# The Newton steps of all norms move from GpSimd to VectorE, in a two-block transformer kernel on one core

## The chip, the cores and the metric

The kernel runs on one core of one Trainium2 chip. The metric is the time of one execution on the device in microseconds (us); lower is better. Before the change it is 1208.56 us, the median of three runs (1205.94, 1208.56 and 1211.92). The trace was taken by the hardware profiler in one further execution. In its rows PE is TensorE's matrix multiplications, PEld its weight loads, DVE is VectorE, ACT ScalarE, POOL GpSimd and SP SyncE, which issues most of the transfers.

## The reference, cut to what matters

256 tokens of 1024 columns pass through two blocks of two layers each, all in float32. The first block mixes tokens by three branches (a recurrent one, attention over selected keys, dilated attention) and then has a gated projection; the second has two kinds of attention, attention to a memory of 256 rows, and a feed-forward layer with a short convolution. Each part begins with a norm over the 1024 columns of a token:

```python
def rms_norm(x, g):
    y = x * lax.rsqrt(jnp.mean(x * x, axis=-1, keepdims=True) + 1e-6)
    return y * g

for i in range(2):                                   # first block
    z = rms_norm(x, norm_g[i]) @ w_in[i]
    x = x + mix(z) @ w_out[i]
    x = x + sigmoid(rms_norm(x, ple_norm_g[i]) @ ple_w_gate[i]) * (p[i] @ ple_w_proj[i])
x = rms_norm(x, final_norm_g)
for l in range(2):                                   # second block
    h = rms_norm(x, attn_norm[l])                    # and, once, rms_norm(x, kv_norm)
    x = x + attention(h, rms_norm(mem, mem_norm[l])) @ w_o[l]
    x = x + conv_ffn(rms_norm(x, ffn_norm[l]), w_up[l], w_down[l])
out = rms_norm(x, final_norm)
```

## The kernel before, in words

The tokens lie in two tiles of 128 rows, `xs[0]` and `xs[1]`. A matrix product in float32 is made of three products of a rounded part and a remainder (`hi` and `lo`, pass list `PASSES`): weights are loaded as `wraw`, ScalarE copies the rounded part into `whi`, and VectorE, or for some blocks GpSimd, subtracts to get `wlo`. Activations are split likewise (tiles `k`, `mT`). Six slots hold weights ahead of their use.

**A norm.** `norm_T` turns a tile of tokens on TensorE into columns, VectorE multiplies by the gains (`zs`), ScalarE and VectorE (or GpSimd) make the two parts. The factor 1/sqrt(mean square) is not applied there; it scales what the products give. `stats` makes it, for each tile of tokens: ScalarE sums the squares (`squares`), VectorE adds the two halves (`halved`, tile `ss`), and `newton` computes the root from an integer seed on VectorE and three rounds of two steps on [128, 1] tiles: `rs_t` = y·y·h, then y = (t - 1.5)·y, in tile `rs_y` (`mrs` for the norm of the memory). Each step needs the one before it. In the kernel before, the steps go to GpSimd unless `newton` is called with `eng=V`, as only the final norm does (`plain_norm`).

The factor is used in two ways: as a column that ScalarE multiplies rows of tokens with, and spread over a square tile: `spread_rs` has VectorE scale the identity by the factor of each tile of tokens (`diag`), then TensorE multiplies the two `diag` with ones, and ScalarE copies the result to `wide`. Between `diag` and the product, `spread_rs` lets other work be issued for a time that is worked out by an estimate, plus `SPREAD_LAG`, 3.5 us.

There are 20 chains of steps on GpSimd, two (one per tile of tokens) for each of: the entry norms of the two first layers, their gate norms (`ple_norm_g`), the memory's norm, the first feed-forward norm, the entry norm of the last layer, and the last feed-forward norm; and four for the norm that joins the first block's final norm with the second's first one (`norm_norm_stats`). In the gate norms GpSimd then halves the factor.

**The order of the work.** Many streams (generators) are emitted by `Flow.run`, which asks an estimate, `Clock`, when the operands of each will be there, and emits next what can go on. The estimate has a price for each instruction and engine (`RATE` and `note`): by them a step of a chain costs 0.15 + 1/475 + 2 x 0.09 = 0.33 us on GpSimd and 0.069 + 1/1920 + 2 x 0.06 = 0.19 on VectorE, plus 0.125 from one to the next. For TensorE the order of emission is the order of execution (`manual_schedule`); that of the other engines is made by the scheduler of the language from the order of emission. GpSimd's other work is weight splits, some `lo` parts of activations, a few products of the recurrent branch, small memsets and the loads of small parameters.

In the rows L458 is the line in `Timed` through which all instructions of VectorE, ScalarE, GpSimd and SyncE are issued, and L616 and L621 are the matrix product and the transpose.

Of the kernel before, what the change touches and what calls it, by code (L numbers as in the profile page):

```python
# [14 lines left out]
ALU = mybir.AluOpType  # L15
AX = mybir.AxisListType
PSUM = bass.MemoryType.PSUM
# [93 lines left out]
class Ev:  # L111
    """A point in the emission that other streams can wait for."""

# [8 lines left out]
class Fork:  # L122
    """A stream to be started that the one that yields it doesn't wait for."""

# [4 lines left out]
WAIT = object()  # L129
# For each run of streams: the time to allow for what may come in between, and that from or to the tensor engine.  # L130
PACE = ((0.2, 0.2), (0.6, 0.28), (0.2, 0.28), (0.5, 0.22), (0.2, 0.2), (0.15, 0.26), (0.2, 0.28), (0.2, 0.2), (0.2, 0.2))
# [5 lines left out]
class At:  # L137
    """The time when some instructions are through, as far as it can be told."""

# [16 lines left out]
class Clock:  # L156
    """Estimates when the engines are through with what has been emitted.

    An instruction's time follows from its size, its dependences from the regions that it reads and writes. An engine
    that is free starts the first of the instructions that are ready. What lies more than PAST before the present  # L160
    is settled for good.
    """

# [20 lines left out]
    def follows(self, pool, old):  # L184
        """Tiles of a pool take the place of those of an earlier one."""
        self.prior[pool] = self.of_pool(old)
# [16 lines left out]
    def before(self, reads, writes=(), lane=None):  # L203
        """The instructions that one with these operands comes after; engines that read a bank of PSUM take turns."""
        deps = []
        for ap in reads:
            if lane and lane != "PE" and ap.space == PSUM:
                deps += [op for other, op in self.last.get(ap.name, {}).items() if other not in (lane, "PE")]
        for aps, write in ((reads, False), (writes, True)):
            for ap in aps:  # L210
                name, p0, p1, f0, f1 = self.region(ap)
                for q0, q1, g0, g1, op, wrote in self.used.get(name, ()):
                    if (wrote or write) and q0 < p1 and p0 < q1 and g0 < f1 and f0 < g1:
                        deps.append(op)
                if write and name not in self.used:
                    deps += self.prior.get(self.pool.get(name), ())
                if write and name in self.owner and name not in self.used:
                    (key, bufs), live = self.owner[name], self.slots.setdefault(self.owner[name][0], [])
                    if len(live) == bufs:
                        deps += self.last[live.pop(0)].values()  # L220
                    live.append(name)
        return deps
# [92 lines left out]
class Flow:  # L315
    """Orders the emission of several streams of work by an estimate of the tensor engine's time.

    A stream is a generator that emits a step at a time and yields what its next step waits for: WAIT (what it has
    emitted), an Ev, an At, 0, or a list of streams to be run before it goes on. Streams given first come first.
    """  # L320

# [30 lines left out]
    def tensor(self, cycles, out, st, mv):  # L352
        """A product of the tensor engine. Those that fill different columns of the array run at the same time.

        The clock is at its full rate in a window that follows one with enough work, counted in full columns.
        """
        lanes = range(*(x // 32 for x in (self.clock.region(out)[1], self.clock.region(out)[2] + 31)))
        t = start = max(self.issue, self.clock.when("PE", self.clock.before((st, mv), (out,))), *(self.lanes[i] for i in lanes))
        share = st.shape[0] / P
        left = cycles  # L360
        while left > 0:
            k = int(t / TICK + 1e-9)
            rate = 2400 if self.work.get(k - 1, 0) >= BUSY else 1200
            n = min(left, max((k + 1) * TICK - t, 1e-6) * rate)
            self.work[k] = self.work.get(k, 0) + n * share
            t += n / rate
            left -= n
        t += 0.0024
        self.issue = start + 0.02
        for i in lanes:  # L370
            self.lanes[i] = t
        self.t = max(self.t, t)
        self.clock.mark(Op("PE", t - start, (), t), (st, mv), (out,))

    def slack(self):
        """Whether the tensor engine has had too little to do of late to keep its clock up."""
        k = int(self.t / TICK)
# [7 lines left out]
    def mine(self, lag=0.0):  # L385
        """What the present stream has emitted, and some time for what may come in between."""
        s = self.cur
# [60 lines left out]
class Timed:  # L448
    """An engine whose instructions the clock sees."""

# [17 lines left out]
class Gate:  # L468
    """Open when some condition holds."""

# [18 lines left out]
def tile_hybrid_stack(ctx: ExitStack, tc: tile.TileContext, a, out):  # L489
# [25 lines left out]
    def load_gains(names):  # L515
        """The gains of norms as columns, a column for each 128 of the rows of the matrices that they scale."""
        n = sum(dict(NORMS)[name] for name in names) * KD
# [163 lines left out]
    class Load:  # L681
        """Weights that are used together, in blocks of what a slot holds."""

# [25 lines left out]
    def loading(u):  # L709
        """Loads and splits weights as slots come free; the units are used in the order in which they are loaded."""  # L710
        if u.after:
# [41 lines left out]
    class Chain:  # L753
        """The weights of a stream in the order of use: the next ones are loaded while some are used."""

# [52 lines left out]
    def proj(mm, n, u, split=False, after=None):  # L808
        """mm makes the products of an output, a row of the weights and its index."""
        for i, b in [(i, b) for b in u.blocks for i in range(n)] if split else [(i, b) for i in range(n) for b in u.blocks]:  # L810
# [58 lines left out]
    class Norm:  # L869
        """The factors of a norm, of which a column scales rows of tokens and the square of a tile columns of tokens."""  # L870

# [13 lines left out]

    def newton(h, tag="rs_y", eng=None):
        """1/sqrt(2 h), with a sign that changes at each step."""
        y = T([P, 1], tag)
        t = T([P, 1], "rs_t")
        ts(y.bitcast(I32), h.bitcast(I32), -0.5, float(0x5F3759DF - (1 << 22) - (1 << 31)), ALU.mult, ALU.add)  # L890
        for _ in range(3):
            ts(t, y, y, h, ALU.mult, ALU.mult, eng or G)
            ts(y, t, 1.5, y, ALU.subtract, ALU.mult, eng or G)
        return y
# [9 lines left out]
    def spread_rs(nr, tag, halves_=False):  # L904
        """The factors along the columns, in all rows."""
        dgs = []
# [25 lines left out]
    def turned_T(xh, t, outs, pool=False):  # L932
        """Puts the transpose of a tile of tokens, scaled by the columns of the gains named in outs, into their stacks."""
        for j in range(2):
# [21 lines left out]
    def norm_norm_stats(x_ev, g1, nr, dst):  # L956
        """xs becomes its norm with g1, and nr has the factors of both that and the norm of it.

        The two factors 1/sqrt(s) and 1/sqrt(q/s + eps), with s and q the mean squares of x (plus eps) and of x g1,
        make 1/sqrt(q + eps s).  # L960
        """
        gb1 = load_gain(g1)
# [31 lines left out]
    def scores(pair):  # L994
        """Of two heads on the two halves of the partitions, whose products the array makes side by side."""
        got = yield from take_n(phase["score"])
# [73 lines left out]
    def scaled(ps, nr, n=2):  # L1070
        """Products of n x 128 rows with tokens along the columns, times the factors of the norm of the tokens."""
        x = T([P, 2, S], "zs")[:, 0:n]
# [11 lines left out]
    def rows(accs, yT, u, t, first, last, toks=None, x_ev=None, turns=True):  # L1084
        """Products of a tile of rows with all the blocks of u, into the two banks in accs, to be added to xs in the end."""
        for b in u.blocks if turns else sorted(u.blocks, key=lambda b: b.cols.start):
# [13 lines left out]
    def out_proj(yT, chain, groups, tags, x_ev):  # L1100
        """Adds the products of a group of rows at a time, so that two banks are enough while the last rows are made."""
        for i, ks in enumerate(groups):
# [1294 lines left out]
    def plain_norm(g, x_ev):  # L2397
        gb = load_gain(g.rearrange("(o n) -> o n", o=1))

        def one(t):  # L2400
# [4 lines left out]
            for j in range(2):  # L2405
                tt(xg[j], xh[j], column(gb)[j], ALU.mult)
            rs = newton(halved(s2), eng=V)
            for j in range(2):
# [123 lines left out]
```

## Time and profile before

| What | Value |
|---|---|
| Median of three runs | 1208.56 us |
| Span of the profiled execution, first to last instruction | 1214.1 us |
| A time of that execution beside its span | not given |
| Instructions | 23478 |
| TensorE busy (products) | 92% |
| VectorE busy | 76% |
| ScalarE busy | 60% |
| GpSimd busy | 30% |
| Mean granted clock of TensorE | 0.956 |

Busy shares are means over the whole span. What one stage loses is read from the waits in that stage: a row such as "PE po <- DVE diag: 5.5, 1, 5.5" says that TensorE stood idle for 5.5 us in total, once, and that the last thing it waited for was VectorE's writing of `diag`. In rows in order of time, a row with x2 joins two instructions that follow closely, its time is that of both, and brackets hold the idle time ahead of it and what ended it. Clock columns give the granted clock of TensorE as a share of 2.4 GHz.

### The profile page before, as it was taken

How to read it: one execution, taken by the hardware profiler on the slowest of the kernel's cores; microseconds unless marked ns; L12 is line 12 of the kernel's file. 1: busy time of each engine (PE TensorE's matmuls, PEld its weight loads, DVE VectorE, ACT ScalarE, POOL GpSimd, SP SyncE). 2: the span in 40 equal slices, each digit the busy share in tenths (PEclk: the TensorE clock that was granted, in tenths of full speed). 3: DMA queues.
4: the chain of work that ended last, by engine and by line, in shares of the span. 5: the costliest groups of instructions: out<-in, count | busy, mean ns of one | idle time of the engine just before them, and what ended most of it. 6: DMA issues, size and time to landing. Idle time of an engine off the chain costs nothing.

```text
span 1214.1 us, 23478 instructions
## 1 busy us (share of the span) xinstructions
PE 1123.1 (92%) x8505; PEld 1000.8 (82%) x8505; DVE 928.3 (76%) x2246; ACT 727.0 (60%) x1642; POOL 362.7 (30%) x355
## 2 busy tenths in 40 slices
PE   6899999988989989979989899999989998999996
PEld 6888887888888867978856899999878867999995
DVE  4889887768898877868777677777777666877786
ACT  4526656656266666666556566666666555766664
POOL 4442213433521226160001612222251124222221
PEclk9879989989899999988979999999989999999999
DMA  7444324444452146647312456666534424666662
GB/s 213 111 125 122 80 53 139 139 140 109 119 141 80 45 134 213 194 116 212 101 35 51 153 152 204 192 187 181 185 92 140 139 84 145 183 191 186 188 183 95
DMA packets 154124, 168.60 MB, mean 139 GB/s; under 512 B 15692, under 2 KB 141532, under 8 KB 154008
## 3 DMA queue, kind: packets, MB, share of 16 engines
q1 hardware_dynamic: 153336, 166.10, 46.9%
q0 software_dynamic: 672, 1.00, 0.4%
q8 instruction: 67, 1.10, 0.4%
q14 instruction: 49, 0.40, 0.1%
HBM read 164.65 MB, written 2.42 MB: 138 GB/s over the span
## 4 chain that ended last, share of the span: by engine, by line
PE 64%; issue 13%; DVE 10%; POOL 8%; ACT 4%; DMA 1%; SPq 0%; ACTq 0%; POOLq 0%; DVEq 0%
PE pz L616 34%; PE po L616 9%; PE pr L616 7%; PE sc L616 7%; POOL k L458 4%; PE tp L616 3%; PE tp L621 3%; POOL wlo L458 2%; DVE k L458 2%; DVE wlo L458 2%; ACT whi L458 2%; POOL rs_t L458 1%; POOL rs_y L458 1%; PE pr L621 1%; DVE zs L458 1%
## 5 line engine op out<-in xcount | busy, mean ns | idle before, releaser
L458 ACT ACTIVATE whi<-wraw 128x512 fp32r<-128x512 f32 (+2 forms) x604 | 371.2, 624 | 248.9 <-PE pz L616 72.5
L458 DVE TENSOR_TENSOR wlo<-wraw,whi 128x512 fp32r<-128x512 f32 (+1 forms) x505 | 365.1, 736 | 141.8 <-ACT whi L458 131.7
L616 PE MATMUL pz<-k,whi 128*128 128x256 f32 x1568 | 314.0, 297 | 7.7 <-ACT k L458 4.9
L616 PEld LDWEIGHTS pz<-k,whi 128*128 128x128 f32 x1568 | 255.8, 200 | 18.5 <-issue 5.8
L458 POOL TENSOR_TENSOR wlo<-wraw,whi 128x512 fp32r<-128x512 f32 (+3 forms) x99 | 132.9, 1344 | 415.9 <-ACT whi L458 378.4
L616 PE MATMUL pz<-whi,k 128*128 128x256 f32 (+5 forms) x1152 | 248.9, 302 | 8.4 <-DVE k L458 5.0
L616 PE MATMUL pz<-k,wlo 128*128 128x256 f32 x784 | 229.1, 292 | 10.2 <-POOL wlo L458 10.2
L616 PEld LDWEIGHTS pz<-whi,k 128*128 128x128 f32 (+1 forms) x1152 | 187.2, 188 | 20.3 <-DVE k L458 6.9
L458 POOL TENSOR_TENSOR k<-yv,k 128x256 fp32r<-128x256 f32 x54 | 95.6, 1785 | 280.8 <-ACT k L458 280.8
L616 PE MATMUL pz<-wlo,k 128*128 128x256 f32 (+5 forms) x576 | 170.6, 296 | 0.1
L616 PEld LDWEIGHTS pz<-k,wlo 128*128 128x128 f32 x784 | 157.2, 200 | 11.5 <-POOL wlo L458 11.5
L616 PE MATMUL po<-k,whi 128*128 128x256 f32 x704 | 132.1, 281 | 0.0
L616 PEld LDWEIGHTS pz<-wlo,k 128*128 128x128 f32 (+1 forms) x576 | 108.5, 188 | 3.3 <-DVE wlo L458 0.6
L616 PEld LDWEIGHTS po<-k,whi 128*128 128x128 f32 x704 | 109.0, 191 | 0.0
L616 PE MATMUL po<-k,wlo 128*128 128x256 f32 x352 | 98.8, 281 | 0.0
L616 PE MATMUL sc<-whi,k 128*128 128x512 f32 x240 | 82.2, 402 | 3.8 <-POOL k L458 3.5
L458 DVE SCALAR_TENSOR_TENSOR k<-zs,convp,k 128x254 f32<-128x254 f32 (+1 forms) x176 | 73.7, 482 | 0.0
L458 ACT ACTIVATE sm<-sm,mn 128x128 f32<-128x128 f32 x100 | 44.4, 445 | 37.9 <-DVE mn L458 37.8
L616 PEld LDWEIGHTS po<-k,wlo 128*128 128x128 f32 x352 | 67.0, 190 | 0.0
L616 PE MATMUL tp<-whi,k 128*128 128x512 f32 x176 | 58.8, 395 | 0.0
L616 PEld LDWEIGHTS sc<-whi,k 128*128 128x128 f32 x240 | 45.1, 189 | 15.9 <-POOL k L458 4.8
L616 PE MATMUL sc<-wlo,k 128*128 128x512 f32 x120 | 47.4, 395 | 0.0
(372 smaller groups left out, 1858.5 us busy)
## 6 DMA issues: line engine op xcount, KB each, us to landing
wraw<-in_w_up_dram SPq DMA_DIRECT2D x88, 512.0 KB
wraw<-in_w_in_dram SPq DMA_DIRECT2D x44, 512.0 KB
wraw<-in_w_down_dram SPq DMA_DIRECT2D x44, 512.0 KB
wraw<-in_w_in_dram SPq DMA_DIRECT2D x32, 256.0 KB
wraw<-in_w_out_dram SPq DMA_DIRECT2D x16, 512.0 KB
wraw<-in_ple_w_gate_dram SPq DMA_DIRECT2D x16, 512.0 KB
wraw<-in_w_o_dram SPq DMA_DIRECT2D x10, 512.0 KB
wraw<-in_w_kv_shared_dram SPq DMA_DIRECT2D x10, 512.0 KB
```

The source lines that it names most:

```text
L458: ins = call(*args, **kw)
L616: nc.tensor.matmul(out_, st, mv, start=start, stop=stop)
L621: nc.tensor.transpose(out_, x, idn)
```

## The change

`newton` loses its argument `eng`, and its steps are issued to VectorE, the default of `ts`. The final norm, which passed `eng=V`, is called without it and stays as it was. The halving of the factor in the gate norms stays on GpSimd (`eng=G` in `stats`). Docstrings and a comment are taken out with the lines kept, so line numbers are the same; this part of the diff is left out here.

```diff
-    def newton(h, tag="rs_y", eng=None):
+    def newton(h, tag="rs_y"):
...
         for _ in range(3):
-            ts(t, y, y, h, ALU.mult, ALU.mult, eng or G)
-            ts(y, t, 1.5, y, ALU.subtract, ALU.mult, eng or G)
+            ts(t, y, y, h, ALU.mult, ALU.mult)
+            ts(y, t, 1.5, y, ALU.subtract, ALU.mult)
         return y
...
-            rs = newton(halved(s2), eng=V)
+            rs = newton(halved(s2))
```

## Rows read from the trace of the kernel before

**Rows 1.** the page, busy time of each engine

```profile
span 1214.1 us, 23478 instructions
...
PE 1123.1 (92%) x8505; PEld 1000.8 (82%) x8505; DVE 928.3 (76%) x2246; ACT 727.0 (60%) x1642; POOL 362.7 (30%) x355
```

**Rows 2.** stretches: us; busy PE, PEld, DVE, ACT, POOL; clock, DMA, GB/s

```profile
545.00:700.00 155.00, 143.29 (x978) 115.54 (x977) 115.54 (x383) 93.71 (x256) 26.44 (x29) 0.90 0.39 111
700.00:886.00 186.00, 183.53 (x1299) 170.41 (x1298) 139.81 (x260) 119.20 (x222) 47.98 (x25) 0.99 0.60 182
```

**Rows 3.** who waited for whom, 510 to 546: us, times, longest

```profile
PE po L616 <- DVE diag L458: 5.5, 1, 5.5
...
PE pz L616 <- POOL wlo L458: 1.4, 1, 1.4
```

**Rows 4.** GpSimd in order of time, first norm of second half

```profile
516.92 1.08 POOL L458 TENSOR_SCALAR rs_t<-rs_y,ss 128x1 f32<-128x1 f32 x2 [4.75 <-DVE rs_y L458]
...
533.53 0.55 POOL L458 TENSOR_SCALAR rs_y<-rs_t,rs_y 128x1 f32<-128x1 f32 x2
```

**Rows 5.** VectorE in order of time, norm before first FFN

```profile
692.31 0.72 DVE L458 TENSOR_TENSOR wlo<-wraw,whi 128x512 fp32r<-128x512 f32 x1 [3.65 <-ACT whi L458]
693.23 1.31 DVE L458 TENSOR_SCALAR diag<-cst,rs_y 128x128 f32<-128x128 f32 x1 [0.20 <-POOL rs_y L458]
```

**Rows 6.** TensorE in order of time, same norm

```profile
694.59 0.80 PE L616 MATMUL po<-diag,ones 128*128 128x128 f32 x2 [3.60 <-DVE diag L458]
```

**Rows 7.** stretches as in rows 2, behind two stalls and in three norms

```profile
535.00:540.00 5.00, 5.00 (x26) 5.00 (x25) 1.36 (x2) 3.85 (x11) 0.60 (x2) 0.53 0.14 30
694.50:698.00 3.50, 3.41 (x16) 3.41 (x17) 0.64 (x2) 0.61 (x2) 0.00 (x0) 0.50 0.70 215
698.00:702.00 4.00, 4.00 (x28) 4.00 (x28) 1.39 (x2) 1.27 (x3) 0.00 (x0) 0.73 0.23 74
466.00:487.00 21.00, 19.58 (x135) 17.08 (x135) 17.32 (x36) 16.90 (x43) 15.58 (x28) 1.00 0.61 189
882.00:900.00 18.00, 13.88 (x70) 11.72 (x69) 14.40 (x24) 10.62 (x24) 13.28 (x18) 0.84 0.28 87
1009.00:1018.00 9.00, 4.45 (x30) 3.59 (x29) 7.85 (x14) 5.79 (x14) 8.70 (x12) 0.98 0.55 171
```

**Rows 8.** groups on GpSimd by form: busy us, mean ns, idle before

```profile
L458 POOL TENSOR_SCALAR rs_t<-rs_y,ss 128x1 f32<-128x1 f32 x54 | 36.4, 677 | 24.9 <-DVE rs_y L458 22.8
L458 POOL TENSOR_SCALAR rs_y<-rs_t,rs_y 128x1 f32<-128x1 f32 x54 | 23.1, 430 | 2.6
```

**Rows 9.** VectorE in order of time, final norm

```profile
1206.44 0.27 DVE L458 TENSOR_SCALAR rs_t<-rs_y,ss 128x1 f32<-128x1 f32 x1
1206.64 0.21 DVE L458 TENSOR_SCALAR ss<-ss 128x1 f32<-128x1 f32 x1
1206.77 0.20 DVE L458 TENSOR_SCALAR rs_y<-rs_t,rs_y 128x1 f32<-128x1 f32 x1
1206.89 0.15 DVE L458 TENSOR_SCALAR rs_y<-ss 128x1 int32<-128x1 int32 x1
...
1208.64 0.27 DVE L458 TENSOR_SCALAR rs_t<-rs_y,ss 128x1 f32<-128x1 f32 x1
...
1209.19 0.49 DVE L458 TENSOR_SCALAR k<-k,rs_y 128x512 f32<-128x512 f32 x1
```

**Rows 10.** instructions on tile diag: min/median/max ns, first and last start

```profile
L458 DVE TENSOR_SCALAR diag<-cst,rs_y x12: 286/290/1307, 18.3 to 1020.0; 128x128 f32<-128x128 f32 x12
```

**Rows 11.** chain that ended last, two steps in both first layers

```profile
28.47 1.49 PE pr L616 x6
...
218.51 4.86 PE pr L616 x21
...
277.06 1.49 PE pr L616 x6
...
462.98 4.88 PE pr L616 x21
```

## The prediction, on record before the changed kernel ran

> **What bounds the kernel now.** I first read the page's table of engines: TensorE is busy for 92% of the span, VectorE for 76%, GpSimd for 30% [rows 1]. So time is saved where TensorE stands still or runs at its lower clock, and it is lost where VectorE, the second fullest engine, holds TensorE up. Next, the stretches: from 700 to 886 us, the first feed-forward block, TensorE is busy for 183.5 of 186 us, so a delay ahead of it goes into the end time whole; from 545 to 700 us it is 143.3 of 155, so part of a gain there can be lost in later waits [rows 2]. Last I asked, around each norm, what TensorE waited for. Two of the norms stop it on what the Newton steps feed.
>
> The first norm of the second half has four chains of steps. GpSimd begins them at 516.92 and ends at 534.08 (533.53 plus 0.55), over 17 us [rows 4], because it works off weight splits in between and because single steps are stretched: the two kinds of step average 677 and 430 ns over the kernel [rows 8]. The last `diag` waits for them, and TensorE, whose order is fixed, waits 5.5 us for `diag`; shortly before, it waited 1.4 us for a split that stood behind the same steps in GpSimd's queue [rows 3]. The norm before the first feed-forward block repeats this: `diag` starts at 693.23 just as GpSimd's last step ends [rows 5], and TensorE waits 3.6 us [rows 6]. Behind either stop the granted clock is low: 0.53 over 5 us after the first, 0.50 over 3.5 and 0.73 over 4 us after the second, against 1.00 at the higher level, 2.4 GHz; 0.50 is the level of 1.2 GHz [rows 7].
>
> **The change, part by part.**
>
> *What leaves GpSimd.* 54 pairs of steps make 18 chains of three pairs [rows 8], and the norm of the memory has 2 more: 20 chains. The final norm has its steps on VectorE already. The steps that GpSimd keeps between are weight splits, halves of `k`, and four halvings of the factor, which now wait for VectorE; I cost those at nothing, since the tanh of the gate that reads them comes after a projection, and without that cover it is one hop between engines in four places, well under 1 us each.
>
> *What a chain costs on VectorE.* The final norm shows the same instructions there. With other work between, a first step holds the queue for 0.20 us (1206.44 to 1206.64) and a second for 0.12 (1206.77 to 1206.89), so a chain takes 3 x 0.32 = 0.98 us from unrounded gaps of about 0.325. Alone, each step waiting for the one before, a pair takes 0.55 us (1208.64 to 1209.19), a chain 1.65 [rows 9]. Twenty chains are 19.6 to 33 us of VectorE, which is what the change can cost at most if nothing hides it.
>
> *Gain at the two stops.* Six chains lie there. First norm: the wait of 5.5, the split's 1.4, and the clock: 5 us of work at 0.53 would take 2.65, so 2.35 more; 9.25 us in all [rows 3, 7]. Will VectorE be in time? The first seeds were there when GpSimd began, at 516.92; TensorE goes on at the latest within a microsecond of GpSimd's end, 534.08, and had then waited 5.5 us, so it came to `diag` at about 529 [rows 3, 4]. That leaves some 12 us for four chains, which even at 1.65 us each take 6.6. After that the first projection and its weights are next late; TensorE's later waits in that stretch (11.7 of 155 us idle [rows 2]) can take some of it back. I take three quarters, 6.9 us; the ends are 0 and 9.25. Norm before the feed-forward block: the wait of 3.6, and of the clock 3.5 x 0.50 + 4 x 0.27 = 2.83; 6.4 us. VectorE stood idle 3.65 us before 692.31 [rows 5], so the steps are hidden there, and the stage behind has 2.5 us of idle TensorE in 186: I take all 6.4; the low end is 3.6, if the clock falls for another reason. Gain 13.3, at most 15.7.
>
> A step can also be held. That `diag` took 1.31 us, while 12 like it have a median of 0.29 [rows 5, 10]: 1.02 us more, at a time when GpSimd worked off weight splits among its steps. One such hold per chain would make the price 0.98 + 1.02 = 2.0 us. On this the Trainium skill has a rule that speaks against the change: its page "SBUF — State Buffer", section "Who interferes with whom", says that VectorE and GpSimd share one pair of ports, that a `tensor_scalar` may take it, and that whoever comes second stands still for the whole instruction of the other. By that rule each new step, a `tensor_scalar` too, can be held behind a split; the one long `diag` agrees, the median doesn't show it as the usual case, and I take 0.98 for the sum and leave 2.0 to the second rival.
>
> *Cost elsewhere.* The other 14 chains sit where VectorE is full. In two norms TensorE starves with it: 882 to 900 us (TensorE 13.9 of 18, VectorE 14.4) and 1009 to 1018 (4.5 of 9, VectorE 7.9) [rows 7]. What queues behind the steps on VectorE are the products with the gains and the lower halves of `k`, and TensorE waits for just these. The two entry norms of the first layers are alike; together 8 chains, 7.8 us if all of it shows. I take half, 3.9: the steps fill gaps in which VectorE waits for ScalarE, and GpSimd's lower halves of `k` no longer stand behind steps. In the two gate norms and the memory's (6 chains; one of the two and the memory's lie in 466 to 487) TensorE is busy 19.6 of 21 us with VectorE at 17.3 [rows 7], since loaded weights keep it going: a sixth of 5.9, 1.0. Cost 4.9; the ends are 0 and 14 x 1.65 = 23.1.
>
> *The order.* An estimate in the kernel decides in which order TensorE's work is issued, and it prices a step at 0.33 us on GpSimd and 0.19 on VectorE, so later streams can interleave otherwise. How much an order is worth: the same layer, between the same two steps, took 218.51 - 28.47 = 190.0 us the first time and 462.98 - 277.06 = 185.9 the second [rows 11]. I put nothing into the sum for this and 4 us either way into the spread.
>
> **The sum.** 1214.1 - 13.3 + 4.9 = 1205.7 us of span in the profiled execution, 0.69% less. No time of it beside its span is shown. Its span is 0.46% above the median of the runs, 1208.56, so I carry the share over: 1208.56 x 1205.7/1214.1 = 1200.2; predicted 1200.
>
> **Rivals.**
>
> *The stops move instead of going (27%).* For it: in both norms weights were being loaded and split at that time, and VectorE's split at 692.31 waited 3.65 us for ScalarE [rows 5], so TensorE may next wait for weights; behind the first norm there are idle times enough to take up a gain [rows 2]. Against it: 183.5 of 186 busy behind the second. With nothing from the first and 3.6 from the second: 1214.1 - 3.6 + 4.9 = 1215.4, or 1209.8 on the median's scale: no change.
>
> *VectorE becomes the bound (17%), the other side.* In the norms where it is full and TensorE waits for its products, the steps run one behind the other at 1.65 us a chain, and all 14 chains show: 1214.1 - 13.3 + 23.1 = 1223.9, 1218.3 on the median's scale. It decides from a price of 13.3/14 = 0.95 us a chain on the path, and reaches 0.5% slower at (13.3 + 6.1)/14 = 1.38. For it: TensorE's idle half in 1009 to 1018 with VectorE at 87%. Against it: 0.98 is the price when other work stands between, and VectorE has that work just where it is full. With one hold per chain, as in the long `diag`, at 2.0 and 28.0 in all: 1228.8, or 1223.1; I give this end 4 of the 17%, since the median of 12 `diag` shows no hold [rows 10]. It is the end that the Trainium skill's rule on the shared ports ("SBUF — State Buffer", "Who interferes with whom") would bring about.
>
> **How the numbers follow.** The forecast, 56%, has a range of its own of 1193 to 1207: 10 to 15.7 us gained, 2 to 8 lost, 4 for the order. About a seventh of it lies above 1202.5, which is 0.5% below the median, about what a measurement of this kernel can tell from no change. So faster: 0.48 + 0.03 of the first rival = 0.51; same: 0.08 + 0.22 + 0.03 of the second = 0.33; slower: 0.14 + 0.02 = 0.16. The range over all cases, 1190 to 1216, reaches above to where the second rival has shown half its price; what lies beyond it on either side is under 2 in 10.
>
> **What would show it.** In the new profile the steps are rows of VectorE with means of 0.2 to 0.3 us, GpSimd is busy some 60 us less (36.4 + 23.1 [rows 8]), TensorE no longer waits for `diag` in either norm, and the clock behind them stays at 1.00. The first rival shows as a wait for `whi`, `wlo` or a load in the same places; the second as longer waits of TensorE for VectorE's `k` around 270, 890 and 1015 us, and as steps of 1 us or more. What would make me wrong is a new order in which TensorE's stops come at other places altogether.

## The result and the profile after

The changed kernel takes 1237.43 us (median of 4 runs, 1233.31 to 1243.93); the kernel before, run beside it, 1209.21 (4 runs, 1205.94 to 1211.92). The ratio is 1.023, 95% interval 1.0201 to 1.026: 2.3% slower. The prediction was 1200 us in a range of 1190 to 1216, so the time lies above the range, and the change goes the other way. The profiled execution took 1233.31 us, 1.8 more than its span. The page's table of engines, which answers to [rows 1]:

```profile
span 1231.5 us, 23489 instructions
...
PE 1122.0 (91%) x8505; PEld 996.2 (81%) x8505; DVE 949.1 (77%) x2366; ACT 729.1 (59%) x1642; POOL 304.4 (25%) x235
```

The work moved as it should: GpSimd is busy 58.3 us less and VectorE 20.8 us more. TensorE does the same work (1122.0 us against 1123.1), so the 17.4 us that the span has grown are idle time of TensorE. (The medians differ by 28.2 us: the execution profiled here is the fastest of its four, and that of before lies above its median, so the two traces show some 60% of the loss.) First the groups on the steps' tile, by form (busy us, mean ns; [rows 8]), and then the instructions on the tiles `rs_t` and `diag` (min/median/max ns; [rows 10]):

```profile
L458 DVE TENSOR_SCALAR rs_t<-rs_y,ss 128x1 f32<-128x1 f32 x60 | 15.2, 265 | 0.4
L458 DVE TENSOR_SCALAR rs_y<-rs_t,rs_y 128x1 f32<-128x1 f32 x60 | 11.4, 205 | 0.4
```

```profile
L458 DVE TENSOR_SCALAR rs_t<-rs_y,ss x60: 254/264/276, 8.6 to 1226.0; 128x1 f32<-128x1 f32 x60
L458 DVE TENSOR_SCALAR rs_y<-rs_t,rs_y x60: 196/204/216, 8.9 to 1226.3; 128x1 f32<-128x1 f32 x60
```

```profile
L458 DVE TENSOR_SCALAR diag<-cst,rs_y x12: 271/285/1174, 14.3 to 1036.6; 128x128 f32<-128x128 f32 x12
```

A step costs what the final norm had shown, 0.26 and 0.20 us, and none of these 120 is stretched. So neither the price of a step nor a hold of it explains the loss. Next, the stretches of the second half's attention and of the first feed-forward block, in the columns of [rows 2]:

```profile
560.00:718.00 158.00, 137.19 (x952) 108.01 (x952) 114.45 (x385) 93.13 (x251) 18.65 (x17) 0.94 0.36 99
718.00:904.00 186.00, 183.63 (x1300) 170.44 (x1299) 140.32 (x261) 118.81 (x221) 49.02 (x25) 0.99 0.59 185
```

TensorE is idle for 20.8 us in the first, where before it was 11.7 of 155; the second is as it was. Next comes what TensorE waits for in the joined norm of the second half (520 to 560 us; [rows 3]). Below it stand two views in order of time of the norm before the first feed-forward block, VectorE's `diag` and then TensorE ([rows 5, 6]):

```profile
PE po L616 <- DVE diag L458: 2.9, 2, 2.0
```

```profile
710.86 0.29 DVE L458 TENSOR_SCALAR diag<-cst,rs_y 128x128 f32<-128x128 f32 x1
```

```profile
709.06 0.39 PE L616 MATMUL pz<-wlo,mT 128*128 128x256 f32 x1 [1.46 <-DVE wlo L458]
715.61 0.50 PE L616 MATMUL pz<-k,whi 128*128 128x256 f32 x2 [2.21 <-ACT mkv L458]
```

In the joined norm TensorE still waits 2.9 us for `diag`, and the granted clock is 0.50 over 541 to 546 us, behind the longer of the two waits. In the second norm the wait of 3.6 us for `diag` is gone, and 1.46 us for a weight split and 2.21 for `mkv` stand in its place. And there is a stop that the kernel before does not have: for the memory norm's `diag`, between 480 and 515 us:

```profile
PE pr L616 <- DVE diag L458: 5.1, 2, 2.6
```

To see where the delay gathers, I took from the order in time of SyncE when the first load of each stage's weights goes out, and subtracted the time of the kernel before. The table is worked out from many rows. A load says how far TensorE has come only if it goes out at the same place of TensorE's order, which the loads of `a_cmp_w` do not: the changed kernel has then begun 4019 of its 8505 products, E2 and E7 4020 and 4025, the kernel before, E1 and E9 4082 or 4083. So two rows go by the start of a product instead, counted from the first, at places where all six kernels have begun the same number of products of each kind. Six kernels that are the same as the kernel before up to `w_in` (E3, E5, E7, E8, E8b, E10) stand between +0.4 and -4.8 there, so a difference of 5 us in a single row can be the execution. From there to the second `w_out`, where they are still the same, they move by less than 2 us.

```
us after the kernel before      changed   E1      E2      E7      E9
first layer (1547th product)     -1.1    +1.8    +4.6    -2.9    +0.3
gate norm through (w_in)         +3.6    +2.5    +8.2    -2.9    +4.7
second layer through (w_out)     +7.1    +8.3   +10.8    -3.2    +9.5
memory norm through (a_w_in)    +14.0   +15.2   +11.8    -3.2   +17.5
attention (4479th product)      +18.1   +13.5   +18.1    +4.9   +12.7
attention through (w_up)        +20.5   +11.5   +27.4   +12.8   +16.3
first FFN through (w_kv_shared) +18.1   +11.2   +26.5   +12.7   +16.1
last w_o                        +18.0   +12.3   +25.9   +13.8   +15.8
```

The changed kernel loses in three places: in the first two layers (it is 7.1 us late there, and more against those six), in the second gate norm and the memory norm (6.9 us), and from the joined norm to the end of the attention stage (6.5 us from `a_w_in` to `w_up`). From the first feed-forward block on nothing is lost, in the last layer's norms either: the span ends 17.4 us later.

### The profile page after: what moved, and what is told of

Its sections match the earlier page's. It is cut to its first block, busy times and chain, and to the rows that moved or that the text cites. A ratio compares the mean times of both kernels' runs of the same rounds, so it can differ in the third digit from the quotient of the medians.

```text
span 1231.5 us, 23489 instructions
## 1 busy us (share of the span) xinstructions
PE 1122.0 (91%) x8505; PEld 996.2 (81%) x8505; DVE 949.1 (77%) x2366; ACT 729.1 (59%) x1642; POOL 304.4 (25%) x235
## 3 DMA queue, kind: packets, MB, share of 16 engines
HBM read 164.65 MB, written 2.42 MB: 136 GB/s over the span
## 4 chain that ended last, share of the span: by engine, by line
PE 55%; DVE 18%; issue 12%; ACT 4%; POOL 4%; DMA 2%; ACTq 0%; POOLq 0%; DVEq 0%; SPq 0%
PE pz L616 28%; PE po L616 9%; PE pr L616 7%; PE sc L616 6%; DVE wlo L458 4%; DVE k L458 4%; PE tp L616 3%; POOL k L458 3%; PE tp L621 2%; ACT whi L458 1%; DVE sm L458 1%; DVE zs L458 1%; ACT k L458 1%; POOL wlo L458 1%; DVE r L458 1%
## 5 line engine op out<-in xcount | busy, mean ns | idle before, releaser
L616 PE MATMUL pz<-k,whi 128*128 128x256 f32 x1568 | 307.2, 293 | 11.6 <-ACT k L458 5.0
L616 PEld LDWEIGHTS pz<-k,whi 128*128 128x128 f32 x1568 | 251.8, 197 | 21.3 <-issue 5.9
L616 PE MATMUL pz<-whi,k 128*128 128x256 f32 (+5 forms) x1152 | 253.5, 305 | 9.9 <-DVE k L458 5.3
L458 POOL TENSOR_TENSOR wlo<-wraw,whi 128x512 fp32r<-128x512 f32 (+3 forms) x99 | 135.7, 1375 | 427.8 <-ACT whi L458 336.3
L616 PE MATMUL pz<-k,wlo 128*128 128x256 f32 x784 | 226.2, 289 | 5.5 <-POOL wlo L458 4.5
L616 PEld LDWEIGHTS pz<-whi,k 128*128 128x128 f32 (+1 forms) x1152 | 190.5, 191 | 22.1 <-DVE k L458 6.6
L458 POOL TENSOR_TENSOR k<-yv,k 128x256 fp32r<-128x256 f32 x54 | 99.0, 1846 | 284.4 <-ACT k L458 284.4
L616 PEld LDWEIGHTS pz<-k,wlo 128*128 128x128 f32 x784 | 154.6, 197 | 6.4 <-POOL wlo L458 5.1
```

What stands on the lines that cost most here:

```text
L458: ins = call(*args, **kw)
L616: nc.tensor.matmul(out_, st, mv, start=start, stop=stop)
```

## The experiments

All ratios are to runs of the kernel before on the same chip, timed beside the run, with 95% intervals. In the edits, `VG` issues to VectorE but tells the planner GpSimd's price, and `GV` the reverse:

```diff
-    lay, cw = _layout()
+    lay, cw = _layout(); VG, GV = Timed(flow, nc.vector, "POOL"), Timed(flow, nc.gpsimd, "DVE")
```

| Run | Steps on VectorE | Planned at VectorE's price | Median, us | Ratio | Interval |
|---|---|---|---|---|---|
| changed kernel | all | all | 1237.43 | 1.0230 | 1.0201 to 1.0260 |
| E1 | all | none | 1221.84 | 1.0103 | 1.0064 to 1.0142 |
| E2 | final norm only | all | 1244.23 | 1.0276 | 1.0237 to 1.0314 |
| E3 | joined norm, first FFN's | none | 1207.98 | 0.9987 | 0.9965 to 1.0008 |
| E4 | all but gate and memory | none | 1214.00 | 1.0031 | 1.0006 to 1.0057 |
| E5 | memory | none | 1214.56 | 1.0032 | 1.0018 to 1.0047 |
| E6 | final norm only; lag 3.0 | none | 1209.02 | 0.9979 | 0.9963 to 0.9996 |
| E7 | final norm only | joined norm | 1229.06 | 1.0140 | 1.0116 to 1.0165 |
| E8 | memory, its product later | none | 1208.78 | 0.9993 | 0.9979 to 1.0007 |
| E8b | final norm only, that product later | none | 1210.78 | 0.9997 | 0.9981 to 1.0014 |
| E9 | all | all but joined norm | 1230.90 | 1.0166 | 1.0129 to 1.0202 |
| E10 | final norm only | half of joined norm | 1221.01 | 1.0089 | 1.0056 to 1.0121 |
| E11 | joined norm, first FFN's; lag 3.0 | none | 1208.60 | 0.9986 | 0.9969 to 1.0003 |
| E12 | entry norms of layers 1, 2 | none | 1217.12 | 1.0061 | 1.0034 to 1.0088 |
| E13 | all, memory's product later | none | 1215.81 | 1.0044 | 1.0024 to 1.0064 |

The final norm's steps are on VectorE in every kernel.

### E1 and E2: the engine without the order, the order without the engine

My first theory was that the new order of TensorE's work did it ("order theory"); the rival was VectorE's load.

```diff
-            ts(t, y, y, h, ALU.mult, ALU.mult, eng or G)
-            ts(y, t, 1.5, y, ALU.subtract, ALU.mult, eng or G)
+            ts(t, y, y, h, ALU.mult, ALU.mult, eng or VG)
+            ts(y, t, 1.5, y, ALU.subtract, ALU.mult, eng or VG)
```

> All 20 chains run on VectorE, but the estimate that orders the emission is told that they cost what they cost on GpSimd; TensorE's instructions then stand in exactly the order of the kernel before. If the new order of TensorE's work is what made the change slower: TensorE's two stops for diag go and the rest stays, 1194 to 1203 us. If VectorE as the bound made it slower: the steps load VectorE as in the changed kernel, 1230 us or more.

E2 has `eng or GV` in the same places.

> All 20 chains run on GpSimd, as in the kernel before, but the estimate is told the price of VectorE; TensorE's instructions then stand in exactly the order of the changed kernel. If the order is the cause: 1235 to 1255 us, since the stops for diag come on top. If VectorE's load is the cause: near the kernel before, 1203 to 1215.

E1 took 1221.84 and E2 1244.23 us. E2 came out as the order theory said: the order alone, with every step back on GpSimd, costs 2.8%. E1 fell between the two forecasts. In TensorE's old order the engine alone costs 1.0%; in the new order it gives 0.5% (1.0230 against 1.0276, intervals that overlap). The order costs 2.8% with the steps on GpSimd and 1.3% with them on VectorE (1.0230/1.0103). Both matter, and they don't simply add.

### E3: only the two norms that were to gain

```diff
-            nr.rs.append(newton(h3))
-            rs1 = newton(h)
+            nr.rs.append(newton(h3, eng=VG))
+            rs1 = newton(h, eng=VG)
...
-        flow.run(norm_T(x2, [(("ffn_norm_2", l), hT2)], True), stats(x2, n2, hT2), *more, ffn(l, hT2, n2, x3))
+        flow.run(norm_T(x2, [(("ffn_norm_2", l), hT2)], True), stats(x2, n2, hT2, eng=VG if l == 0 else None), *more, ffn(l, hT2, n2, x3))
```

> Only the six chains of the two norms that stop TensorE (the norm at the start of the second half, and the first feed-forward norm) run on VectorE; order of TensorE as in the kernel before. Both theories, the order and VectorE's load, expect the gain of the two stops here, 1193 to 1200 us; what separates this run from the one with all chains on VectorE in the same order is what the other 14 chains cost VectorE: about nothing by the order theory, 20 us or more by the load theory.

Both theories missed: 1207.98 us, no change that the interval shows, though TensorE's order is the old one and only these steps were moved. Some rows of VectorE in order of time, in the joined norm:

```profile
517.09 0.21 DVE L458 TENSOR_SCALAR rs_y<-ss 128x1 int32<-128x1 int32 x2
...
519.95 0.44 DVE L458 TENSOR_SCALAR rs_t<-rs_y,ss 128x1 f32<-128x1 f32 x2
520.31 1.29 DVE L458 TENSOR_TENSOR k<-zs,k 128x512 fp32r<-128x512 f32 x1
...
521.65 0.32 DVE L458 TENSOR_SCALAR rs_y<-rs_t,rs_y 128x1 f32<-128x1 f32 x2
521.89 0.20 DVE L458 TENSOR_SCALAR rs_y<-ss 128x1 int32<-128x1 int32 x2
...
522.81 1.75 DVE L458 TENSOR_TENSOR wlo<-wraw,whi 128x512 fp32r<-128x512 f32 x1
...
530.28 0.21 DVE L458 TENSOR_SCALAR rs_y<-rs_t,rs_y 128x1 f32<-128x1 f32 x1
530.41 1.36 DVE L458 TENSOR_TENSOR wlo<-wraw,whi 128x512 fp32r<-128x512 f32 x2
531.68 0.21 DVE L458 TENSOR_SCALAR rs_y<-rs_t,rs_y 128x1 f32<-128x1 f32 x1
531.80 0.28 DVE L458 TENSOR_SCALAR diag<-cst,rs_y 128x128 f32<-128x128 f32 x1
```

The steps are 0.2 to 0.27 us each, but between many of them VectorE has a whole `wlo`, `k`, `zs` or `mT` of 0.7 to 1.75 us in its order. From the first step to `diag` it takes 11.85 us for four chains that need 6.6 by themselves. Some 1.7 us of that is work in between that took longer than usual: the `k` at 520.31 and the `wlo` at 522.81 took 1.29 and 1.75 us, others like them 0.69, while GpSimd made weight splits from 518.05 to 524.01. The two chains of the second tile of tokens can't start before their seeds, at 521.89, and end 9.9 us later. TensorE, in order of time, there and in the norm before the feed-forward block:

```profile
532.14 0.80 PE L616 MATMUL po<-diag,ones 128*128 128x128 f32 x2 [4.18 <-DVE diag L458]
...
692.52 0.51 PE L616 MATMUL pz<-k,whi 128*128 128x256 f32 x2 [2.44 <-ACT mkv L458]
```

ScalarE in order of time in the second norm, in E3 and then in the kernel before, and last TensorE in the kernel before:

```profile
691.11 0.63 ACT L458 ACTIVATE whi<-wraw 128x512 fp32r<-128x512 f32 x1 [2.32 <-DMA wraw<-in_w_up_dram]
691.65 0.82 ACT L458 ACTIVATE mkv<-pz,mrs 128x256 f32<-128x256 f32 x2
```

```profile
692.19 0.82 ACT L458 ACTIVATE mkv<-pz,mrs 128x256 f32<-128x256 f32 x2
```

```profile
695.40 0.78 PE L616 MATMUL pz<-k,whi 128*128 128x256 f32 x2
```

It still stops 4.18 us for the joined norm's last `diag` (5.5 before), and the granted clock behind it is 0.53 over 5 us as before. In the second norm `diag` was written at 687.60 (before, 693.23; the execution stood some 3 us ahead by then), and TensorE stopped 2.44 us for the next thing in its order, `mkv`. That stands on ScalarE behind a `whi` that had waited 2.32 us for its load of `w_up`. The kernel before had `mkv` ready at 693.01 (692.19 plus 0.82) and began the product that waits for it in E3 at 695.40, so at most some 2.4 us could be gained there while that load lands when it does. What E3 gains, it gains in the joined norm: where the load of `a_cmp_w` has the old place, it shows E3, E1, E4, E9 and E13, with these four chains on VectorE, gaining 3.1 to 4.2 us after the load of `a_w_in`, and E5 and E12, with them on GpSimd, 0.1 at most. The theory that came of it, the latency theory: VectorE works in order, so a chain ends when the work placed between its steps is done, and where TensorE has its product soon, that latency is what costs.

### E4 and E5: which chains lose

E4 is E1 with `eng=G` in the gate norms' `stats` and in the memory norm; E5 has only this edit:

```diff
-                nr.rs.append(newton(halved(s2), "mrs"))
+                nr.rs.append(newton(halved(s2), "mrs", VG))
```

> The Newton steps of the two gate norms and the memory norm (6 chains) stay on GpSimd, the other 14 chains are on VectorE, and TensorE's order is that of the kernel before. Latency theory (a chain on VectorE waits its turn in that engine's order at each of its seven instructions, so its end comes late where TensorE has a product for it soon): the 6.9 us that the run with all chains on VectorE lost between the second layer's w_out and w_mem_kv come back, so 1212 to 1217 us. Load theory (the steps cost what they add to VectorE's busy time, and these 6 chains hold 36 of the 114 steps moved): a third of the 11 us, so 1217 to 1220 us.

> Only the memory norm's two chains are on VectorE (12 steps, 2.8 us of work), TensorE's order is that of the kernel before. Latency theory: TensorE stops for the memory norm's diag for some 5 us, as in the run with all chains on VectorE, and the time is 4 to 7 us over the kernel before, 1213 to 1218 us. Load theory: under 1 us, so 1209 to 1212 us.

Both came out as the latency theory said: 1214.00 and 1214.56 us. (E4 keeps back 36 of 120 steps, not of 114.) Twelve steps with 2.8 us of work cost 0.32%, 3.9 us. VectorE in order of time, the two chains' first and last instructions, in E5 and in the kernel before, and then TensorE in E5:

```profile
471.86 0.14 DVE L458 TENSOR_SCALAR mrs<-ss 128x1 int32<-128x1 int32 x1
...
490.80 0.29 DVE L458 TENSOR_SCALAR diag<-cst,mrs 128x128 f32<-128x128 f32 x1
```

```profile
473.47 0.14 DVE L458 TENSOR_SCALAR mrs<-ss 128x1 int32<-128x1 int32 x1
...
486.73 0.28 DVE L458 TENSOR_SCALAR diag<-cst,mrs 128x128 f32<-128x128 f32 x1 [0.70 <-POOL mrs L458]
```

```profile
487.68 0.49 PE L616 MATMUL pr<-diag,ones 128*128 128x128 f32 x2 [1.18 <-DVE diag L458]
491.14 0.80 PE L616 MATMUL pr<-diag,ones 128*128 128x128 f32 x2 [2.98 <-DVE diag L458]
```

The chains take 19 us on VectorE from first seed to last `diag`. With the steps on GpSimd, in the kernel before, it was 13 us, and TensorE had no wait for it.

### E8, E8b and E13: the same chains, the product later

If it is latency, giving the chain time must heal it, with all steps still on VectorE. E8 is E5 with this edit, E8b has this edit alone, E13 is E1 with it:

```diff
-        yield flow.mine(SPREAD_LAG)
+        yield flow.mine(SPREAD_LAG + (8 if tag == "mwide" else 0))
```

> Only the memory norm's two chains are on VectorE, and the planner leaves 11.5 instead of 3.5 us between this norm's diag and its product, so that TensorE has the product later in its order. Latency theory: TensorE no longer stops for that diag, and the time is within 2 us of the kernel with the same order and the chains on GpSimd. Load theory: the 4 us that these chains cost on VectorE stay, whatever the place of the product: 3 to 5 us over that kernel.

> The control: all chains on GpSimd, with the memory norm's product at the same later place in TensorE's order. Both theories: within 3 us of the kernel before, 1208 to 1214 us, since the kernel before does not stop there.

> All 20 chains on VectorE, planned at GpSimd's price, and the memory norm's product 8 us later in TensorE's order; otherwise that order is the one of the kernel before. Latency theory: the 5 to 7 us lost at the memory norm come back, 1214 to 1218 us against 1222 with the product in its old place. Load theory: unchanged, 1220 to 1224 us.

All three as the latency theory said: 1208.78 against the control's 1210.78 us, and all chains on VectorE fall from 1.0103 to 1.0044. In E8 the last `diag` is even later than in E5, and the products run without a wait (VectorE's row, then TensorE's):

```profile
492.70 0.28 DVE L458 TENSOR_SCALAR diag<-cst,mrs 128x128 f32<-128x128 f32 x1
```

```profile
494.49 0.61 PE L616 MATMUL pr<-diag,ones 128*128 128x128 f32 x4
```

### E12: the entry norms of the first two layers

In E1 and E4 some 3 us or more were lost in the second layer's attention, where no norm stands.

```diff
-        flow.run(entry(), stats(x_ev, n1, hT), first_params(l, rw, hT), rwkv_chain(l, rw, yT), sparse_attn(l, sp, yT), sparse_turn(sp), dense())
+        flow.run(entry(), stats(x_ev, n1, hT, eng=VG), first_params(l, rw, hT), rwkv_chain(l, rw, yT), sparse_attn(l, sp, yT), sparse_turn(sp), dense())
```

> Only the four chains of the entry norms of the first two layers are on VectorE, with TensorE's order that of the kernel before. ScalarE's order differs in two places behind them, where gth goes ahead of a copy of the scores, which the run with 14 chains on VectorE showed as a stop of 1.9 us on that copy in the second layer. If that order is what cost that run 3 us in the stage: 2 to 4 us over the kernel before, 1212 to 1215 us. If these norms cost nothing but VectorE's time: 1209 to 1212 us.

It took 1217.12 us, 0.61% more and above both forecasts: these norms cost more than VectorE's time, and more than the first theory had put on ScalarE's order. TensorE's waits for the copy of the scores, in the first layer's attention (110 to 180 us) and in the second's (370 to 400), are not there in the kernel before:

```profile
PE sc L616 <- ACT k L458: 3.3, 1, 3.3
...
PE sc L616 <- ACT k L458: 1.9, 1, 1.9
```

ScalarE at the second place, in order of time, in E12 and then in the kernel before:

```profile
376.87 0.42 ACT L458 ACTIVATE gth<-zs 128x256 f32<-128x256 f32 x1 [2.42 <-DVE zs L458]
377.19 0.58 ACT L458 ACTIVATE k<-sc 128x512 f32<-128x512 f32 x1
```

```profile
376.56 0.60 ACT L458 ACTIVATE k<-sc 128x512 f32<-128x512 f32 x1
377.06 0.41 ACT L458 ACTIVATE gth<-zs 128x256 f32<-128x256 f32 x1
```

The order on VectorE, ScalarE and GpSimd is made by a scheduler of the language with its own estimate of time. With four chains moved, it puts a `gth` ahead of the copy `k<-sc`, that `gth` waits 2.42 us for VectorE, and the copy that TensorE wants stands behind it. It does so some 100 us after the norm, in both layers. That this order is the cause is read from the rows; no run puts ScalarE's order back with the steps left on VectorE. Between the loads of `w_in` and `w_out` around the second place E12 loses 3.4 us, and what it loses at the first place is for the most part made good by the end of that layer. And it holds in TensorE's old order alone: E1 and E4 have the same two stops, the changed kernel and E9 have neither. E4, with these chains and eight more on VectorE, lost 0.31% (0.06 to 0.57), so the price is best put at 0.3 to 0.6%.

### E6, E7, E9 and E10: where the order loses

```diff
-    GN_LAG, SPREAD_LAG, GRAM_LAG = 2.0, 3.5, 2.0
+    GN_LAG, SPREAD_LAG, GRAM_LAG = 2.0, 3.0, 2.0
```

is E6. E7 gives the joined norm's four chains VectorE's price (`newton(h3, eng=GV)`, `newton(h, eng=GV)`), E10 the two of `h3` alone; E9 is the changed kernel with `eng=VG` for these four.

> All steps on GpSimd as in the kernel before; one constant of the planner, the time that it leaves between a norm's diag and its product, is 3.0 instead of 3.5 us, which moves those products to other places in TensorE's order. If the time depends on the order in that any other order is worse than this one, 1220 to 1245 us as with the new prices. If the new prices of the steps did it by themselves, 1205 to 1215 us.

> All steps run on GpSimd, but the planner is given VectorE's price for the four chains of the joined norm between the halves alone; TensorE's order is that of the kernel before up to there, and another after it. If the loss in the attention stage of the second half (15 to 20 us in both kernels planned with VectorE's price) comes from the orders that follow from this norm's price: 1222 to 1235 us, with the stage from a_w_in to w_up longer by 10 us or more. If it comes from orders that were set before, under 1215 us.

> The changed kernel (all steps on VectorE, planned at VectorE's price), but the joined norm's four chains are planned at GpSimd's price, so that TensorE's order differs from that of the changed kernel from that norm to the end of the attention stage of the second half alone. If that order is what cost the changed kernel 15 us in this stage: 1217 to 1225 us, with the stage from a_w_in to w_up shorter by 10 us or more. If it was VectorE's load in the stage: 1234 to 1240 us.

> All steps on GpSimd; the planner is given VectorE's price for two of the joined norm's four chains (those of the factor h3). If the order in the attention stage turns with the place of the norm's end by small steps, half of the 18 us lost with all four chains priced so: 1215 to 1224 us. If it is a switch between orders, either 1206 to 1214 or 1225 to 1235 us.

E6 (1209.02) shows that a different order need not be worse: it is 0.2% faster. But it is a small difference: compared place by place, its order of products departs from the old one in some 40 of 8505 places, that of the changed kernel in some 2500. E7 (1229.06) shows that the price of one norm's steps, with no step moved, is worth 1.4%. By the table it loses 16.0 us from `a_w_in` to `w_up` (-3.2 to +12.8). Its attention stage, in the columns of [rows 2], and TensorE in order of time:

```profile
545.00:700.00 155.00, 136.31 (x908) 106.12 (x907) 109.56 (x371) 90.30 (x245) 19.67 (x21) 0.90 0.33 93
```

```profile
564.10 0.42 PE L621 MATMUL pz<-cst,k 30*128 30x30 f32 x2 [5.07 <-DVE k L458]
...
592.47 0.61 PE L621 MATMUL tp<-cst,sm 128*128 128x128 f32 x3 [2.07 <-DVE sm L458]
```

The changed kernel, in order of time, has the first of these stops too:

```profile
577.53 0.41 PE L621 MATMUL pz<-cst,k 30*128 30x30 f32 x2 [4.68 <-DVE k L458]
```

TensorE is busy 7 us less in the same 155 us than in [rows 2]. The longest stop of E7 there is 5.07 us for a `k` of VectorE; it is 4.68 in the changed kernel and 4.8 in E2, the other two with the joined norm at VectorE's price, against 1.88 in the kernel before and 1.8, 1.6 and 3.1 in E1, E9 and E3, with the old price. The rest goes into shorter waits, such as the one for a softmax tile. E10 (1221.01) lies between, as the forecast of small steps had it. E9 missed: 1230.90 and not 1217 to 1225. Without the joined norm's price the changed kernel gets back 0.6%, not 1.4. The table shows as much: from `a_w_in` to `w_up` the changed kernel loses 6.5 us and E9 gains 1.2, so that this price costs 7.7 us with the steps on VectorE, half of the 16.0 that it costs in E7 with them on GpSimd. What is left of the order's cost, 0.6% over E1 (the intervals overlap), the table does not place. E2 places more of it: with every step on GpSimd it is 10.8 us late by the second layer's `w_out`, so the new order costs in the first two layers as well. Which decisions of the planner do this was not settled.

### E11: a version from the parts that did not lose

E3 with E6's lag.

> A version put together from the parts that did not lose: the six chains of the two norms forecast to gain on VectorE (the joined norm between the halves and the first FFN's norm), planned at GpSimd's price, with the planner's lag at 3.0 instead of 3.5 us; all other chains on GpSimd. Latency theory: the gains of the two parts (0.13% and 0.21% in their own runs) add, 1205 to 1209 us. Load theory: the same.

1208.60 us, 0.14% faster with an interval that includes no change. No version tried beats the kernel before by an amount worth keeping.

## Why the prediction was wrong

*The steps' price* was right: 0.265 and 0.205 us, VectorE 20.8 us busier, near the lower end of 19.6 to 33. GpSimd fell by 58.3 us as forecast.

*"Will VectorE be in time?"* is the first step that failed. It gave four chains 6.6 us behind one another and found 12 us of room. In E3 they took 11.85 us, because the step took the time that a chain needs alone for the time that it takes in a full queue. The room was wrong too: it was counted from the first tile's seeds, but the second tile's come at 521.89 and TensorE was at their `diag` by 527.96, which leaves 6.1 us for two chains that took 9.9. GpSimd's own 17 us [rows 4] had shown such a delay, and I read it as a trait of GpSimd. Of the gain of 13.3 us, E3 got 1.6 (0.13%), with an interval that includes none; of the 6.9 in the joined norm, the traces show 3.1 to 4.2.

*The norm before the feed-forward block*: `diag` did come early, and the first rival happened there. What was late next was `mkv`, which I had not named, but it was late behind a weight that was still being loaded, as the rival had it. The argument against it, 183.5 of 186 us busy behind the stop, spoke of the stage after it and not of the next instructions in TensorE's order. The gain was put at 6.4 us, and with `mkv` ready at 693.01 no more than some 2.4 was there.

*The gate and memory norms*, put at 1.0 us because TensorE was busy 19.6 of 21 us there [rows 7]: the memory norm alone costs 3.9 us (E5), and from E4 to E1 all six chains 0.7%; in the changed kernel the stop for that `diag` is 5.1 us. A busy TensorE at GpSimd's latency says nothing of a latency 6 us longer. By E8 and E13 it is latency and not VectorE's time, for the memory norm; the gate norms were not run apart.

*The entry norms and those of the last layer* were put at 3.9 us as time of VectorE. In the last layer nothing was lost (from `w_kv_shared` to the last `w_o` the table moves by 0.1 us, and the span ends 17.4 us later). In the first two layers, in TensorE's old order, the four chains cost 0.3 to 0.6%, and the rows point to ScalarE's order, for which the sum has no term. The changed kernel doesn't have those stops. What it loses there is lost in E2 too, which has its steps on GpSimd, so it is put down to the next term.

*The order*, put at 0 with 4 us either way, is the second step that failed and the largest error: 2.8% by itself (E2), and still 1.3% with the steps on VectorE (the changed kernel over E1). The spread was taken from one layer run twice in one order, which says how much a stage's surroundings vary and not what another order costs. The last sentence on what would make the forecast wrong, stops at other places, is in the main what happened.

*The rivals.* "VectorE becomes the bound" gave a time on the right side, 1218.3 or 1223.1 us, but not by its mechanism: VectorE is 77% busy, no step is stretched, and the last layer's norms cost nothing. The hold of a step behind a split did not occur: the longest of 60 is 0.276 us. It occurs with `diag`. One of them took 1.17 us while GpSimd made lower halves of `k`; both rows in order of time, VectorE and GpSimd:

```profile
914.60 1.17 DVE L458 TENSOR_SCALAR diag<-cst,rs_y 128x128 f32<-128x128 f32 x1
```

```profile
912.72 2.97 POOL L458 TENSOR_TENSOR k<-zs,k 128x512 fp32r<-128x512 f32 x2 [3.40 <-ACT k L458]
```

`diag` ends at 915.77, GpSimd's second product at 915.69. Two steps in the same stretch, at 913.46 and 914.48, took 0.20 us each. The Trainium skill's rule on the shared ports ("SBUF — State Buffer", "Who interferes with whom") agrees with this row for a tile of 128 columns; for the steps, of one column, the runs show nothing of it. So taking the steps off GpSimd did not take the long `diag` away.

Put together in ratios, in TensorE's old order: the gate and memory norms 0.3 to 0.7%, the entry norms 0.3 to 0.6, the two norms of the forecast -0.1, against 1.0 for all (E1). The new order adds 1.3.

## What to carry to other kernels

A chain of short dependent instructions that is moved to a full engine with a fixed order can cost far more in latency than in work, as here: count what its queue holds between two steps, and set that against when the consumer wants the result, or move the consumer later with it, as E8 did. Where a planner or a scheduler orders the work by estimated durations, a change of engine is also a change of order on every engine, far from the place of the edit; measure it apart, by running one thing and planning with the price of the other. When a stop is removed, look up the next instruction in that engine's order and when its inputs were ready in the old trace, since that is where the gain can end. And before a load is used as a mark of progress, check that it stands at the same place of the order in both kernels.

## What the runs showed of the hardware

A `tensor_scalar` on one column took 0.254 to 0.276 and 0.196 to 0.216 us on VectorE over 60 of each, some of them beside GpSimd's products; on GpSimd the same steps had means of 0.677 and 0.430 [rows 8]. A `diag` of 128 columns on VectorE was stretched from 0.285 to 1.17 us beside a GpSimd product, with no Newton step on GpSimd. In E3, behind a stop of 4.18 us TensorE's granted clock was 0.53 over the next 5 us (532 to 537), near the level of 1.2 GHz, and 1.00 over the 5 after that; behind one of 2.44 us it was 0.74 over 691.5 to 698.
